# The order of transposes and gates within a chunk of a hybrid decoder's first stage

## The chip, the cores and the metric

The kernel runs on one core of one Trainium2 chip. The metric is the time of one execution on the device in microseconds, as the median of several runs. The core has a matrix engine (TensorE, PE in the rows; PEld is its weight load), a vector engine (VectorE, DVE), an activation engine (ScalarE, ACT), GpSimd (POOL) and SyncE (SP), which here issues all transfers. Each engine works through its own queue in order.

## What is computed

The reference is one inference step of one decoder layer with two groups of heads beside each other. For a prompt of 4096 positions with 1024 features (and 8 sample rows with one position each):

```
xn    = rms_norm(x, norm_pre)
proj  = xn @ w_in                    # 2304 columns, split into
x_rnn, g_rnn, q, k, v, g_att = split(proj)
xc    = causal_conv(x_rnn)           # width 4, per channel
r, i  = sigmoid(blockdiag(w_ga, xc) + b_ga), sigmoid(blockdiag(w_gx, xc) + b_gx)
a     = exp(-8 r softplus(-lam))
h_t   = a_t h_{t-1} + sqrt(1 - a_t^2) (i_t xc_t)
mix   = concat(h * silu(g_rnn), window_attention(q, k, v) * silu(g_att))
y     = x + rms_norm(mix @ w_out, norm_post)
```

Also returned are the last states of the convolution, the recurrence and the attention window. All is in float32; the kernel splits each operand of a product into a high and a low part and adds three products of them.

## The kernel before, in words

The work has three stages. **Stage A** does the norm, the transposes of the features, the projections of the recurrent half (eight tiles of 128 columns of `w_in`), the convolution, the gates and the scan. **Stage B** does the other projections and the attention, **stage C** the output projection. A and B go over the prompt in 11 chunks: the first has 256 positions and the 8 sample rows, the other ten 384 positions. The change lies in stage A alone.

Within stage A a chunk is a list of items, written out in `A_ORDER` (line 32) and worked off by the loop at lines 429 to 448. With `ci` the chunk and `c` one of the four channel tiles of the recurrent half:

- `P c` is `proj_A` (line 277): two projections side by side, the input and the SiLU gate of channel tile c (`project2`, line 190, with `mm3`, lines 123 to 125): 8 tiles of features, 2 outputs, 3 products, so 48 matmuls over 384 columns into two PSUM tiles of the tag `mm`, which has four. ACT then reads the first one twice (`xr`, line 286, and `xc`, line 290), VectorE adds three taps (line 292) and splits the result (`xk`, lines 300 and 301; 2 buffers); ACT takes the tanh of the second (line 304) and VectorE makes `sg` of it (line 306; 5 buffers).
- `R c` is `rnn_A` (line 309): six gate matmuls from `xk` into the one PSUM tile `gt` (lines 123 to 125 with `gt` as output), four activations on ACT (lines 321, 322, 325, 326), four operations on VectorE (lines 327 to 330).
- `L` is `load_A` (line 146) of chunk ci+1: for three tiles of 128 positions a transfer (line 154; the tag `xs` has 4 buffers), a sum of squares on ACT (line 162), a power and a scaling on POOL (lines 142 and 167).
- `X c` is `prep_A` (line 171) of chunk ci+1 for the feature tiles 2c and 2c+1: three transposes into a PSUM tile each (line 177; the tag `t` has 2), the high part on ACT (`xh`, line 180), the low part on VectorE (`xl`, line 181), and both parts sent to DRAM for stage B (line 183). `xh` and `xl` have 12 buffers each, and a chunk holds 8.
- `S` is `scan_A` (line 333) of chunk ci-1: one square root over all four channel tiles on ACT (line 336), which needs another activation table than the tanh and the exponential, then on VectorE a product, a scan and the product with `sg` for each channel tile (lines 338, 340, 349), and the transfers of line 350.

The loop of stage A, cut to the items:

```
for ci in range(NCH):
    for item in A_ORDER:
        f, s = item[0], st[ci]
        c = int(item[1:] or 0)
        if f == "P":
            s["p", c] = proj_A(pa, ci, c, wA, s["x"])
        elif f == "R":
            ...
            s["r", c] = rnn_A(pa, ci, c, s["uu"], *s["p", c])
        elif f == "S":
            ...
            scan_A(pa, ci - 1, s["uu"], [s["r", c] for c in range(4)])
        elif ci + 1 < NCH:
            if f == "L":
                s["n"] = load_A(prep, ci + 1)
            else:
                ...
                prep_A(ci + 1, s["n"], (2 * c, 2 * c + 1), x)
```

The text's order is not the order of an engine's queue. The program is built in a `TileContext` with `schedule_with_timeline_sim=True` (line 1020): a planner plays the program through at build time, with durations of its own. On each engine it takes, among the instructions whose inputs and buffers are ready in that play, the one that stands earliest in the text. A later item thus fills a gap of an earlier one. The queues that come out are fixed, and the chip's real durations do not change them.

Where stage A ends, its PSUM and SBUF pools are given to stage B (lines 722 to 728); eight tiles of `w_in` for stage B take the buffers of stage A's weights, and two more those of the pool `pa_late`, which holds `hh` among others.

Of the kernel before, what the change touches and what calls it, by code (L numbers as in the profile page):

```python
# [28 lines left out]

A_ORDER = "P1 S L P0 P2 R1 X0 R0 P3 X1 R2 X2 R3 X3".split()

B_FIRST = "V Q0 K Q1 U00 U01 Q2 Q3 G0 U02 U10 G1 U11 U12 M00 M01 G2 G3 M02 X M10 M11 M12".split()
B_ORDER = "Q0 Q1 K Q2 V U00 U01 Q3 U02 U10 G0 U11 G2 G1 M00 M01 M02 U12 G3 M10 M11 M12 X".split()
# [9 lines left out]
def hymba_kernel(ctx: ExitStack, tc: tile.TileContext, ins, outs):  # L45
# [70 lines left out]
    def load_w_in(m, pool=None, bufs=None, spare=None, eng=nc.vector, fast=False):  # L116
        return load_w(w_in_v[:, :, m * P:(m + 1) * P], f"in{m}", pool or wpool, bufs, spare, eng, fast)
# [97 lines left out]

    AORDER = [m for item in A_ORDER if item[0] == "P" for m in (int(item[1]), 4 + int(item[1]))]
    wA = {m: load_w_in(m, eng=nc.gpsimd, fast=True) for m in AORDER[:2]}
# [211 lines left out]
# [3 lines that stand above are left out]
# [603 lines left out]
```

## Time and profile before

| | us |
|---|---|
| median of 3 runs | 1421.48 (1420.98 to 1422.85) |
| the profiled execution's own time | 1416.61 |
| span of the profiled execution | 1414.5 |
| PE busy in the span | 1366.8 (97%) |
| VectorE busy | 1023.1 (72%) |
| ACT busy | 829.9 (59%) |
| POOL busy | 445.0 (31%) |

Stage A lies between about 15 and 463 us of the span, stage B begins beside its end, and stage C ends at 1414.5 us. All tables of the section on rows are of this one execution. "Busy" of PE counts pipelined matmuls up to their modelled ends, so a matmul's duration (0.33 us) is about twice its distance to the next.

### The profile page before, as it was taken

The numbers are of one execution on the slowest core, as the hardware profiler recorded it, in microseconds if no ns is written. First come the engines' busy times: TensorE is split into PE (matmuls) and PEld (weight loads), VectorE is DVE, ScalarE is ACT, GpSimd is POOL, SyncE is SP. The second block draws the span as 40 slices with busy tenths as digits, with TensorE's granted clock in tenths as the row PEclk, the third lists the DMA queues.
The fourth block names the chain that finished last, engine by engine and source line by source line (L and its number), as shares of the span: only waits on it lengthen the run. The fifth ranks groups of instructions, "written<-read, shape, count | busy, mean of one in ns | idle before, by whom it ended". The sixth has DMA issues, their size and how long they took to land. (4 is left out here: it accounts for less than half of the span.)

```text
span 1414.5 us, 23962 instructions
## 1 busy us (share of the span) xinstructions
PE 1366.8 (97%) x7983; PEld 1290.1 (91%) x7983; DVE 1023.1 (72%) x2421; ACT 829.9 (59%) x2095; POOL 445.0 (31%) x876
## 2 busy tenths in 40 slices
PE   5999999999999879999999999999999999999998
PEld 4999989999999879999999999999998887788886
DVE  6778877878778776566576665665676798888874
ACT  4666656756656666676675775766777443333431
POOL 3233332223421023544543534545435110000000
PEclk9999999999999999999999999999999999999999
DMA  8423453433337430331312303303134665345542
GB/s 265 146 96 140 146 173 133 148 121 133 127 120 203 142 120 9 120 113 61 101 51 73 101 13 113 102 13 112 57 103 133 201 198 166 127 158 176 170 157 90
DMA packets 139013, 174.42 MB, mean 123 GB/s; under 512 B 12646, under 2 KB 120758, under 8 KB 138890
## 3 DMA queue, kind: packets, MB, share of 16 engines
q1 hardware_dynamic: 138890, 172.90, 37.5%
q8 instruction: 63, 1.03, 0.3%
q14 instruction: 60, 0.49, 0.1%
HBM read 104.38 MB, written 68.50 MB: 122 GB/s over the span
## 5 line engine op out<-in xcount | busy, mean ns | idle before, releaser
L124 PE MATMUL pr<-xl,wh_in 128*128 128x384 f32 (+1 forms) x688 | 229.7, 335 | 0.0
L125 PE MATMUL pr<-xh,wl_in 128*128 128x384 f32 (+1 forms) x688 | 227.8, 333 | 0.0
L123 PE MATMUL pr<-xh,wh_in 128*128 128x384 f32 (+1 forms) x688 | 218.1, 337 | 8.3 <-ACT xc L290 8.3
L123 PEld LDWEIGHTS pr<-xh,wh_in 128*128 128x128 f32 x688 | 128.1, 188 | 10.1 <-ACT xc L290 9.8
L606 ACT ACTIVATE tt<-tt,nm 128x129 f32<-128x129 f32 x256 | 99.9, 393 | 61.4 <-DVE nm L603 61.2
L124 PEld LDWEIGHTS pr<-xl,wh_in 128*128 128x128 f32 x688 | 129.4, 188 | 0.7 <-issue 0.7
L125 PEld LDWEIGHTS pr<-xh,wl_in 128*128 128x128 f32 x688 | 129.3, 188 | 0.0
L123 PE MATMUL pq<-xh_B,wh_in 128*128 128x384 f32 (+1 forms) x352 | 117.7, 335 | 1.8 <-ACT qz L550 1.1
L123 PE MATMUL pga<-xh_B,wh_in 128*128 128x384 f32 (+1 forms) x352 | 118.3, 336 | 0.7 <-ACT qz L550 0.7
L124 PE MATMUL pga<-xl_B,wh_in 128*128 128x384 f32 (+1 forms) x352 | 118.0, 335 | 0.0
L124 PE MATMUL pq<-xl_B,wh_in 128*128 128x384 f32 (+1 forms) x352 | 117.9, 335 | 0.0
L125 PE MATMUL pq<-xh_B,wl_in 128*128 128x384 f32 (+1 forms) x352 | 117.9, 335 | 0.0
L125 PE MATMUL pga<-xh_B,wl_in 128*128 128x384 f32 (+1 forms) x352 | 117.2, 333 | 0.0
L292 DVE SCALAR_TENSOR_TENSOR xc<-xr,cT,xc 128x384 f32<-128x384 f32 (+1 forms) x132 | 87.3, 677 | 6.8 <-ACT xc L290 6.5
L633 POOL TENSOR_SCALAR_AFFINE_SELECT p<-ph 64x256 fp32r<-64x256 f32 x124 | 53.1, 429 | 103.0 <-PE po L640 82.1
L123 PEld LDWEIGHTS pq<-xh_B,wh_in 128*128 128x128 f32 x352 | 66.8, 190 | 2.4 <-ACT qz L550 1.4
L655 POOL TENSOR_TENSOR mxb<-mxb,sgb 128x256 f32<-128x256 f32 x64 | 47.1, 741 | 67.3 <-DVE mxb L648 64.0
L321 ACT ACTIVATE thr<-gt,hba 128x384 f32<-128x384 f32 (+1 forms) x44 | 25.2, 573 | 72.3 <-PE gt L125 71.4
L123 PEld LDWEIGHTS pga<-xh_B,wh_in 128*128 128x128 f32 x352 | 66.7, 190 | 0.9 <-ACT qz L550 0.9
L125 PEld LDWEIGHTS pq<-xh_B,wl_in 128*128 128x128 f32 x352 | 66.9, 190 | 0.3 <-issue 0.2
L124 PEld LDWEIGHTS pq<-xl_B,wh_in 128*128 128x128 f32 x352 | 66.9, 190 | 0.1
L124 PEld LDWEIGHTS pga<-xl_B,wh_in 128*128 128x128 f32 x352 | 66.8, 190 | 0.0
(764 smaller groups left out, 4100.2 us busy)
## 6 DMA issues: line engine op xcount, KB each, us to landing
xs<-in_x_prompt_dram SPq DMA_DIRECT2D x32, 512.0 KB
xr<-in_x_prompt_dram SPq DMA_DIRECT2D x32, 512.0 KB
out_dram<-xr SPq DMA_DIRECT2D x31, 512.0 KB
xT_d<-xh SPq DMA_DIRECT2D x80, 192.0 KB
xT_d<-xl SPq DMA_DIRECT2D x80, 192.0 KB
xh_B<-xT_d SPq DMA_DIRECT2D x80, 192.0 KB
xl_B<-xT_d SPq DMA_DIRECT2D x80, 192.0 KB
mix<-mix_d SPq DMA_DIRECT2D x30, 512.0 KB
```

Of the source, the lines that this page charges most:

```text
L123: nc.tensor.matmul(out, wh, xh, start=first, stop=False)
L124: nc.tensor.matmul(out, wh, xl, start=False, stop=False)
L125: nc.tensor.matmul(out, wl, xh, start=False, stop=last)
L292: nc.vector.scalar_tensor_tensor(xc[:, :npt], xr[:, t:t + npt], cw[:, t, c:c + 1], xc[:, :npt], op0=ALU.mult, op1=ALU.add)
L321: act(thr, pg[:, 0:W], AF.Tanh, scale=0.5, bias=hba[:, c:c + 1])
L606: act(tt[:, g, 0:P + 1], tt[:, g, 0:P + 1], AF.Exp, scale=-1.0, bias=nm[:, g:g + 1], accum_out=sm[:, g:g + 1])
L633: nc.gpsimd.affine_select(dst, src[r, :, r], pattern=[[0, 4], [-1, HD]], compare_op=ALU.is_gt, fill=0.0, base=0, channel_multiplier=1)
L655: nc.gpsimd.tensor_mul(oo, oo, st["sg", kv][:, :, b * P:(b + 1) * P])
```

## The change

Only the order of the items changes. P1 S L P0 P2 stays; X0 goes ahead of R1, X1 ahead of R0, X2 and X3 stand around P3 where R0, X1 and R2 stood, and R2 and R3 come last.

```diff
-A_ORDER = "P1 S L P0 P2 R1 X0 R0 P3 X1 R2 X2 R3 X3".split()
+A_ORDER = "P1 S L P0 P2 X0 R1 X1 R0 X2 P3 X3 R2 R3".split()
```

`AORDER` (line 216), the order in which stage A's weights are loaded, is taken from the P items and stays 1, 0, 2, 3. For the last chunk X and L are empty.

## Rows read from the trace of the kernel before

**Rows 1.** The page, part 1: busy time and share of the span, by engine.

```profile
PE 1366.8 (97%) x7983; PEld 1290.1 (91%) x7983; DVE 1023.1 (72%) x2421; ACT 829.9 (59%) x2095; POOL 445.0 (31%) x876
```

**Rows 2.** Busy time by stretches: one chunk, and the handover to stage B.

```profile
core 0: us, PE busy (x) PEld busy (x) DVE busy (x) ACT busy (x) POOL busy (x), PEclk, DMA share, GB/s
...
239.60:279.70 40.10, 40.07 (x238) 39.83 (x239) 33.47 (x67) 25.91 (x44) 10.27 (x18) 1.00 0.39 137
...
470.00:515.00 45.00, 32.16 (x213) 29.83 (x212) 37.04 (x101) 32.69 (x84) 3.17 (x9) 0.89 0.17 53
```

**Rows 3.** Waits of PE, 40 to 440 us: us in total, times, longest.

```profile
PE pr L123 <- ACT xc L290: 6.8, 5, 1.6
PE pt L177 <- POOL xs L167: 0.4, 1, 0.4
```

**Rows 4.** Timeline around one stall: start, us, engine, line, operation [idle before].

```profile
400.07 1.28 ACT L336 ACT_TABLE_LOAD   x1
...
401.36 1.49 ACT L336 ACTIVATE uu<-uu 128x1536 f32<-128x1536 f32 x1
...
403.79 0.47 ACT L286 ACTIVATE xr<-pr 128x384 f32<-128x384 f32 x1
404.16 0.66 ACT L290 ACTIVATE xc<-pr,cT 128x384 f32<-128x384 f32 x1
...
404.88 0.44 PE L123 MATMUL pr<-xh,wh_in 128*128 128x384 f32 x1 [1.58 <-ACT xc L290]
```

**Rows 5.** Timeline of PE around the end of a chunk's P3, before that stall.

```profile
371.36 0.42 PE L123 MATMUL pr<-xh,wh_in 128*128 128x384 f32 x1
...
380.89 0.82 PE L177 MATMUL pt<-ident,xs 128*128 128x128 f32 x6
...
392.66 0.34 PE L123 MATMUL gt<-xk,gwh 128*128 128x384 f32 x1
...
395.09 0.49 PE L177 MATMUL pt<-ident,xs 128*128 128x128 f32 x3
```

**Rows 6.** Timeline of PE: six transposes between matmuls of a projection.

```profile
229.34 0.82 PE L177 MATMUL pt<-ident,xs 128*128 128x128 f32 x6
229.92 0.42 PE L124 MATMUL pr<-xl,wh_in 128*128 128x384 f32 x1
230.18 0.33 PE L125 MATMUL pr<-xh,wl_in 128*128 128x384 f32 x1
```

**Rows 7.** Groups of ACT, 40 to 440 us.

```profile
L180 ACT ACTIVATE xh<-pt,gpre 128x384 fp32r<-128x384 f32 x80 | 43.8, 584 | 22.0 <-PE pt L177 22.0
...
L326 ACT ACTIVATE thr<-thr,sp4n 128x384 f32<-128x384 f32 (+1 forms) x40 | 28.1, 702 | 0.9
...
L321 ACT ACTIVATE thr<-gt,hba 128x384 f32<-128x384 f32 (+1 forms) x40 | 22.9, 572 | 72.2 <-PE gt L125 71.4 <-DVE xl L181 0.7
```

**Rows 8.** Groups of VectorE, 40 to 440 us.

```profile
L292 DVE SCALAR_TENSOR_TENSOR xc<-xr,cT,xc 128x384 f32<-128x384 f32 (+1 forms) x117 | 78.1, 685 | 6.8 <-ACT xc L290 6.5 <-POOL xh L288 0.2
L181 DVE SCALAR_TENSOR_TENSOR xl<-pt,gpre,xh 128x384 fp32r<-128x384 f32 x80 | 47.6, 611 | 11.7 <-ACT xh L180 11.5
```

**Rows 9.** Timeline of SP's queue: loads of three tiles for a later chunk.

```profile
353.01 1.31 SPq L154 DMA_DIRECT2D xs<-in_x_prompt_dram  x3
```

**Rows 10.** Timeline of POOL: scaling of the second of those tiles.

```profile
366.08 1.84 POOL L167 TENSOR_SCALAR xs<-xs,rs 128x1024 f32<-128x1024 f32 x1
```

**Rows 11.** Timeline of VectorE: the first product with `sg` in a chunk's scan.

```profile
409.46 1.12 DVE L349 TENSOR_TENSOR hh<-hh,sg 128x384 f32<-128x384 f32 x1
```

**Rows 12.** Timeline of PE at the handover: waits of over 2 us.

```profile
475.32 0.44 PE L123 MATMUL gt<-xk,gwh 128*128 128x384 f32 x1 [2.86 <-ACT thi L322]
...
504.63 0.66 PE L614 MATMUL pT<-ident,tt 128*128 128x128 f32 x4 [2.24 <-DVE tt L611]
...
508.82 0.77 PE L623 MATMUL po<-ph,vs 128*128 128x512 f32 x1 [3.53 <-ACT ph L618]
```

**Rows 13.** Timeline of ACT at the handover: the wait ahead of two weight tiles.

```profile
506.09 2.00 ACT L112 ACTIVATE wh_in<-ws_in 128x1024 fp32r<-128x1024 f32 x2 [3.69 <-DMA mix_d<-hh]
```

## The prediction

> **What bounds the kernel now.** The page first: PE is busy for 97% of the span [rows 1], so only its idle time and the small costs between its matmuls can be won, 47.7 us in all. The next view is the busy time by stretches. It shows where this idle time is not: a chunk of stage A without a stall lasts 40.1 us and PE is busy in 40.07 of them, at the full granted clock (1.00, 2.4 GHz) [rows 2]. It is also not in POOL or SP, which PE hardly ever waits for.
>
> The waits of PE between 40 and 440 us then say what ends its idle time in the middle of stage A: 6.8 us in front of projections, five waits released by ACT's `xc`, and 0.4 us in front of transposes, released by POOL [rows 3].
>
> The timeline of the longest shows the mechanism [rows 4]. PE waits at 404.88 for a PSUM tile that `xr` and `xc` still read. These stand in ACT's queue behind the square root of the scan and its table load (400.07 to 402.85). That alone would not matter: a projection pair has two of four `mm` tiles, so while P0 runs, P1's are read. But here P1 and P0 end together, so all four are full. The reason is in PE's timeline [rows 5]. P3 of the old chunk ends at 380.89, and only then do X1's six transposes run; X3's last three run at 395.09, 14.2 us after P3. Until then P1 lacks its last feature tiles, P0 is taken as filler with what is there, and both finish after X3.
>
> **The change, part by part.** Write c for a chunk. Nothing is added or removed: per chunk 192 projection matmuls, 24 gate matmuls, 24 transposes, and the same work on every other engine, four transfers on SP for each X included.
>
> *X0 to X2 go ahead of P3, X3 right behind it.* X0 needs the scaled tiles `xs`. Their loads are issued at 353.01, when X3 has read the tiles before, and the second of them is scaled by 367.92, 14.9 us later [rows 9, 10]; the first two X's of the next chunk would now be due 25 us and more after X3, so the 0.4 us POOL wait goes too. In P3's window PE has 48 + 12 (R1, R0) matmuls at 0.176 us (54 took the 9.53 us from 371.36 to 380.89 [rows 5]) and three X's of 0.58 us [rows 6], 12.3 us. ACT has in it six `xh`, eight activations of R1 and R0 (at 0.57 and 0.70) and P2's reading: 3.5 + 5.1 + 1.6 = 10.2 us [rows 4, 7]. VectorE has six `xl` (3.7 us), three taps (2.1 us) and eleven other passes over a tile of the same size; taking each at the 0.61 us of `xl`, too much rather than too little, 6.7 us: 12.5 us [rows 8]. So VectorE is about full, and X2 and X3 may slip a little behind P3. `xh` and `xl` of X2 and X3 also need buffers that P3 is the last to read (12 for 8 + 8), which come free tile by tile as P3 goes. I take X3 as done 2 us after P3.
>
> *What follows for P1 and P0.* With all feature tiles there, P1 takes its 48 matmuls first, R2 and R3 among them, and ends some 11 us after P3; P0 ends 8.4 us later. In these 8.4 us ACT has to read P1's tiles. At worst the root stands ahead of it with both table loads, 2 x 1.28 + 1.49 = 4.1 us, then `xr` and `xc`, 1.1 us [rows 4]: 5.2 us, so P2 finds its tiles free. X3 would have to be done later than about 8 us after P3 to bring the stall back. Taken out: all five stalls, -6.8 us; bounds 0 and -6.8. With the POOL wait, -0.4.
>
> The page "ScalarE: Activation LUTs" of the Trainium skill, section "What ACT_TABLE_LOAD costs", speaks against this ease: it gives a table switch 2.66 us, the load and a drain. By it the root's block would be an estimated 6.8 us, with `xr` and `xc` 7.9, and hardly anything of P0's 8.4 us would be left, so that one sum of squares in between would keep part of each stall and the sum would lose up to some 6 us. The rows show the load alone: the root starts 1.29 us after its load began [rows 4], and I go by that.
>
> *Transposes between matmuls.* Six take 0.58 us wherever they stand, and the matmul behind them 0.42 us in place of 0.33 [rows 6]: 0.09 us for each return to matmuls. X0 now comes in two or three pieces and would come in one, X1 to X3 may come in three to six. One return less in two of three chunks, out of nine, is -0.5 us; bounds -1.5 and +1.5.
>
> *R2 and R3 last.* R0 now runs after P3 and R3's first matmul at 392.66, 11.8 us after it [rows 5]. With R1 and R0 inside P3, R3 waits only for P3's own taps, about 6 us. So the scan's start comes about 6 us sooner. The gates' own cost, 24 x 0.176 us, does not change, and P1 covers R3's wait.
>
> *The handover to stage B.* In the last chunk there is no X, but P1 there still ends with P0, and all four gates come behind P3. One of them is waited for (2.86 us), and the first attention units wait 2.24 and 3.53 us [rows 12], the last one because ACT stands before a weight tile whose buffer the scan's output holds until it is sent, 3.69 us [rows 13]. PE is idle for 12.8 of 45 us there, and the clock is at 0.89 on average, so part of the stretch ran at the lower level, 1.2 GHz [rows 2]. With P1 early, R1 and R0 move into P3, and the last scan follows P3 sooner. How much of the idle time goes, no row shows, as VectorE is busy for 37.0 of the 45 us: bounds -8.6 us (those three waits) and +3.5 us (one more such wait). I take half of the gain, -4.0, as the gate wait goes first.
>
> **The sum.** -6.8 - 0.4 - 0.5 - 4.0 = -11.7 us. Against the profiled execution, 1416.61 us in a span of 1414.5, this is 1404.9 us. The median of the runs, 1421.48, lies 4.9 us above that execution; with the same difference the median is 1409.8 us, -0.8%. A measurement can tell about 0.2%, 2.8 us, from no change.
>
> **The rivals.**
> *The handover gives all it has*, the three waits of 8.6 us: -16.3 us, 1405.2 us. For it speaks that all three hang on the last gates and the scan; against it, VectorE's load.
> *The stalls stay*: if the planner, with durations of its own, places X3 still 8 us or more behind P3, P1 and P0 end together as before. For it speaks that the planner spaces gates widely, ACT waits 71 us for them [rows 7], and that VectorE is nearly full in P3's window. Then the handover stays too, and the time is about 1421 us.
> *A smaller stall stays*: the root with its two loads and a sum of squares end up ahead of `xr` and `xc`, and each takes longer than its row. If P2 still waits 0.6 us in nine chunks, that is 5.4 us given back, 1415.2 us. The rows speak against it, with 5.2 of 8.4 us [rows 4]. The page's 2.66 us for a switch would bring it about.
> *Slower, a new wait at P3's first matmul.* `sg` has five buffers, so P0's takes the place of one that the last scan must have multiplied. That product starts at 409.46, 28.6 us after P3 [rows 5, 11]; with P0's own pass at 0.6 us its PSUM tile is free at about 29.8 us. In the new order P3 is due after 156 matmuls and six transposes, 28.0 us. If the scan came no sooner than now, P3 would wait 1.8 us in nine chunks, 16.2 us; less the 7.2 us of stalls, 1430.5 us. It decides where R3, now behind X3 and R2 in the text, gains less than 1.8 us; I count on 6.
>
> **How the numbers follow.** Forecast 0.52, handover in full 0.14, smaller stall 0.05, stalls stay 0.17, new wait 0.12. The forecast's own range, with the bounds of the returns and the handover, is 1404 to 1418 us. The range reaches from 1403 to 1421 us, over the first four cases, and leaves out the slower one. Faster by over 0.2% are the first three, 0.71; within it the fourth, 0.17; slower the last, 0.12.
>
> **What would show it.** Right: no wait of PE on `xc` between 40 and 440 us; X1 and X2 inside P3 and X3 within 3 us of its end; P1's 48 matmuls done well before P0's; chunks of 40 us throughout. R3 within 7 us of P3, and at the handover no gate wait. Wrong: transposes still 7 us or more behind P3; a wait of P3 or P2 on `sg`, line 306; idle time after 470 us as long as now or longer, whatever the chunks do.

## The result, and the profile after

The changed kernel takes 1405.47 us (median of 5 runs, 1400.21 to 1407.19) against 1421.48 us before: 16.0 us less, a ratio of 0.9877 with a 95% interval of 0.9862 to 0.9893. Forecast were 1409.8 us in a range of 1403 to 1421, so the sign is right and the size 4.3 us short. The profiled execution took 1400.21 us with a span of 1398.5, against 1416.61 and 1414.5 before, so the two spans, 16.0 us apart, may be compared: each is the fastest execution on record of its kernel.

The page, part 1, of the changed kernel (busy time, share of the span, instructions):

```profile
PE 1364.4 (98%) x7983; PEld 1292.2 (92%) x7983; DVE 1016.5 (73%) x2421; ACT 829.8 (59%) x2095; POOL 463.5 (33%) x876
```

PE's busy time has hardly changed, 1364.4 against 1366.8 us [rows 1]; what went is mostly idle time, 34.1 in place of 47.7 us. Where it went is seen by cutting both spans at two places: the end of the last projection of stage A (462.6 us before, 453.0 after), and the first scores of stage B's second chunk (538.9 and 521.9). I call the piece between them the handover. Busy time by stretches, of the kernel before and then of the changed one; the columns are us, PE, PEld, DVE, ACT, POOL, PE's granted clock, DMA share, GB/s:

```profile
40.00:462.60 422.60, 415.39 (x2488) 409.52 (x2487) 330.46 (x668) 262.56 (x453) 127.99 (x188) 1.00 0.42 142
462.60:538.90 76.30, 63.32 (x418) 60.30 (x418) 53.93 (x137) 48.51 (x123) 13.88 (x32) 0.93 0.34 109
```

```profile
40.00:453.00 413.00, 412.82 (x2477) 408.82 (x2477) 325.30 (x669) 264.53 (x454) 144.55 (x187) 1.00 0.44 146
453.00:521.90 68.90, 60.51 (x421) 59.41 (x420) 50.51 (x131) 44.78 (x118) 13.62 (x31) 0.95 0.36 115
```

Stage A ends 9.6 us sooner. PE's idle time in it is 0.2 us in place of 7.2. The handover is 7.4 us shorter: PE's idle time falls from 13.0 to 8.4 us there, and the granted clock rises from 0.93 to 0.95. Of the 17.0 us won by then, 1.0 comes back in the stages behind. There the clock of this execution is at 0.51 from 1060.6 to 1064.0 us, with PE busy for 3.35 of the 3.4 us, which costs it 1.7 us; between 538.9 us and the last 3 us of the kernel before it never falls.

The waits of PE between 40 and 440 us (us in total, times, longest), where five stalls on `xc` stood [rows 3]:

```profile
PE pr L123 <- DVE sg L306: 0.2, 1, 0.2
```

The stalls and the POOL wait are gone. The one wait left, 0.2 us on `sg`, is at the place of the prediction's slower rival.

PE's timeline around the end of a chunk's P3, in the changed kernel (start, us, engine, line, operation), to be held against [rows 5]:

```profile
374.48 0.82 PE L177 MATMUL pt<-ident,xs 128*128 128x128 f32 x6
375.05 0.42 PE L125 MATMUL pr<-xh,wl_in 128*128 128x384 f32 x1
375.31 0.34 PE L123 MATMUL gt<-xk,gwh 128*128 128x384 f32 x1
...
380.04 0.49 PE L177 MATMUL pt<-ident,xs 128*128 128x128 f32 x3
...
380.90 0.49 PE L177 MATMUL pt<-ident,xs 128*128 128x128 f32 x3
...
382.62 0.34 PE L123 MATMUL gt<-xk,gwh 128*128 128x384 f32 x1
```

X2 lies inside P3, whose last matmul is at 375.05 and which ends at 375.31, where R2 follows. X3 runs at 380.04 and 380.90, and R3 begins at 382.62. X3's last three transposes come 5.6 us after P3's end, where they came 14.2 us after it. From 384.75 us on PE runs 106 projection matmuls without a break. Of these 12 are P1's and 46 P0's, so P1 ends a whole 8 us ahead of P2.

ACT's timeline in the same chunk shows what became of the block that held `xr` back [rows 4]:

```profile
385.15 1.06 ACT L162 ACTIVATE sq<-xs 128x1024 bf16<-128x1024 f32 x1 [3.14 <-DMA xs<-in_x_prompt_dram]
...
387.73 0.49 ACT L286 ACTIVATE xr<-pr 128x384 f32<-128x384 f32 x1
388.10 0.68 ACT L290 ACTIVATE xc<-pr,cT 128x384 f32<-128x384 f32 x1
...
390.64 1.06 ACT L162 ACTIVATE sq<-xs 128x1024 bf16<-128x1024 f32 x1 [0.88 <-DMA xs<-in_x_prompt_dram]
...
391.81 1.28 ACT L336 ACT_TABLE_LOAD   x1
393.10 1.50 ACT L336 ACTIVATE uu<-uu 128x1536 f32<-128x1536 f32 x1
394.55 0.49 ACT L286 ACTIVATE xr<-pr 128x384 f32<-128x384 f32 x1
```

P1's tile is read at 387.73, 5.4 us before the root (393.10), and only P0's stands behind it. The sums of squares `sq` (line 162) still wait for the loads of the raw tiles, 3.14 us here and 30.8 us between 40 and 440 us against 12.1 before; from 40 us on PE waits for nothing behind them any more.

The waits of PE in the handover, 453.0 to 521.9 us:

```profile
PE pga L123 <- ACT qz L550: 3.7, 1, 3.7
PE pga L123 <- DVE sgb L561: 3.2, 2, 2.7
PE pq L123 <- DVE ksT L510: 1.5, 1, 1.5
```

The three long waits of [rows 12], 8.6 us, and ACT's wait of [rows 13] are gone. Beside them stood 4.3 us of other waits; now these others are 8.4 us.

### The profile page after: what moved, and what is told of

Same layout as the page of the kernel before. It is cut to its first block, busy times and chain, and to the rows that moved or that the text cites. A ratio compares the mean times of both kernels' runs of the same rounds, so it can differ in the third digit from the quotient of the medians.

```text
span 1398.5 us, 23988 instructions
## 1 busy us (share of the span) xinstructions
PE 1364.4 (98%) x7983; PEld 1292.2 (92%) x7983; DVE 1016.5 (73%) x2421; ACT 829.8 (59%) x2095; POOL 463.5 (33%) x876
## 5 line engine op out<-in xcount | busy, mean ns | idle before, releaser
L123 PE MATMUL pr<-xh,wh_in 128*128 128x384 f32 (+1 forms) x688 | 227.1, 334 | 1.1 <-ACT xc L290 0.9
L283 POOL COPY xr<-xh 128x3 f32<-128x3 f32 x40 | 49.5, 1239 | 125.4 <-DVE xc L292 98.5
L292 DVE SCALAR_TENSOR_TENSOR xc<-xr,cT,xc 128x384 f32<-128x384 f32 (+1 forms) x132 | 80.5, 611 | 11.6 <-POOL xh L288 7.4
L180 ACT ACTIVATE xh<-pt,gpre 128x384 fp32r<-128x384 f32 (+1 forms) x88 | 47.4, 576 | 51.3 <-PE pt L177 51.1
L619 DVE TENSOR_TENSOR pl<-pT,ph 128x512 fp32r<-128x512 f32 x64 | 44.0, 688 | 33.1 <-PE po L640 23.4
```

What stands on the lines that cost most here:

```text
L123: nc.tensor.matmul(out, wh, xh, start=first, stop=False)
L180: act(h, pt[:, :W], AF.Copy, scale=gpre[:, k:k + 1])
L283: nc.gpsimd.tensor_copy(xr[:, 0:3], xrprev[c])
L292: nc.vector.scalar_tensor_tensor(xc[:, :npt], xr[:, t:t + npt], cw[:, t, c:c + 1], xc[:, :npt], op0=ALU.mult, op1=ALU.add)
```

## The experiments

My theory after the result: the stalls went because X3 comes early, so that P1 ends ahead of P0; and the handover gained because the last chunk's P1 ends early, which chunk 9's order sets. Each run below is compared with the kernel before; runs 3, 6, 7, 8, 9, 11 and 12 are edits of the changed kernel, the others of the kernel before. Times are medians over executions, but waits and stretches are those of the one profiled execution. The handover of runs 6 and 7, whose chunks have the changed kernel's order, takes 70.2 and 69.8 us in place of 68.9, so I read nothing into a difference of 1 to 2 us.

**1. The gates alone.**

```diff
-A_ORDER = "P1 S L P0 P2 R1 X0 R0 P3 X1 R2 X2 R3 X3".split()
+A_ORDER = "P1 S L P0 P2 R1 X0 R0 P3 X1 X2 X3 R2 R3".split()
```

> Only R2 and R3 are put behind X2 and X3; the X items keep their places of before, so X3 still ends some 13 us after P3 (88 matmuls and transposes behind it) and P1 and P0 end together. Theory (it is the transposes' places that count): stalls of P2 on xc as before, 5 to 9 us in all, the handover as before, time 0.997 to 1.003 of the kernel before. Rival (it is the gates' places that count): stalls gone and the scan sooner, 0.995 or less.

Measured: 1414.47 us, ratio 0.9949 (0.9933 to 0.9964); three stalls, 3.9 us in all; handover 74.7 us. Neither theory has this: the stalls stay, and yet 6.7 us are won. Where these lie stays open. The trace can't say, as the profiled execution was the slowest of the ten (1420.72 us, 4.1 us more than that of the kernel before), and in it stage A ends 2.9 us later than before although the stalls are 2.9 us shorter.

**2. One item alone.**

```diff
-A_ORDER = "P1 S L P0 P2 R1 X0 R0 P3 X1 R2 X2 R3 X3".split()
+A_ORDER = "P1 S L P0 P2 R1 X0 R0 X1 P3 R2 X2 R3 X3".split()
```

> One item alone moves from the order of before: X1 goes from behind P3 to ahead of it. X3 then ends 53 matmuls and transposes after P3 (36 in the changed kernel, 84 to 88 before) and P1 ends 33 of them, some 6 us, ahead of P2. Theory: 6 us are enough for the root's block of 5.2 us, so the stalls are gone or below 1.5 us, and the handover gains as P1 of the last chunk is early too; 0.987 to 0.992 of the kernel before. Rival (X2 ahead of P3 and the gates behind are needed): stalls of 3 us or more stay, 0.994 or more.

Measured: 1408.87 us, ratio 0.9900 (0.9875 to 0.9924). One wait on `xc` of 0.3 us is left and stage A ends at 454.6 us. The handover takes 74.7 us: at most 1.6 us of the 7.4 are there. So X1 ahead of P3 is enough for 8.0 of stage A's 9.6 us, and the early end of P1 in the last chunk is not enough for the handover.

**3. The order of before in chunk 9.**

```diff
+A_OLD = "P1 S L P0 P2 R1 X0 R0 P3 X1 R2 X2 R3 X3".split()
...
-        for item in A_ORDER:
+        for item in A_OLD if ci == NCH - 2 else A_ORDER:
```

> The changed order in every chunk but 9, which has the order of before; chunk 9 makes the feature tiles of the last chunk, so P1 and P0 end together there and the gates of the last chunk come behind P3. Theory: the gain of stage A's chunks stays (8 to 9.5 us), that of the handover (7.4 us) goes, as it hangs on P1 of the last chunk: 0.993 to 0.995 of the kernel before, with the gates of R3 15 us or more behind P3's end. Rival (the handover gains because stage A ends sooner and its queues are emptier, whatever chunk 9 does): 0.987 to 0.990.

Measured: 1414.83 us, ratio 0.9939 (0.9915 to 0.9963). No stall on `xc` after the first chunk, and the handover, by busy time:

```profile
457.60:536.00 78.40, 64.26 (x412) 61.46 (x411) 52.73 (x133) 47.81 (x123) 12.81 (x31) 0.91 0.32 103
```

78.4 us: the whole gain of the handover is gone, as the theory said, and the clock with it, 0.91. The changed order in chunk 9 is needed for it.

**4. A root without a table.** The scan's root is replaced by a scaled copy, so the root is left out of what is computed.

```diff
-        act(uu[:, :, :W], uu[:, :, :W], AF.Sqrt, scale=-0.25)
+        act(uu[:, :, :W], uu[:, :, :W], AF.Copy, scale=-0.25)
```

> The kernel before, with the scan's square root replaced by a scaled copy, which needs no table of its own (the root is left out of what is computed); PE's order in the chunks is that of before, X3 still 13 us behind P3. Theory (stalls come from xr and xc behind the root and its two table loads, once P1 and P0 end together): the block is some 2.6 us shorter, the stalls were at most 1.6 us each, so they are gone or below 1 us in all, and the handover gains 0 to 3 us; 0.993 to 0.996 of the kernel before. Rival (two projections that end together stall P2 by themselves): stalls of 5 us or more stay, 0.998 to 1.000.

Measured: 1416.21 us, ratio 0.9956 (0.9935 to 0.9977). The time is as expected, the stalls are not: three of five went, two stayed with 4.1 us, one of them longer (2.97 us) than any before. The 2.7 us of stalls are not all of the 4.9 us won; the rest stays open. At that place ACT shows what stands ahead of `xr`:

```profile
73.58 1.06 ACT L162 ACTIVATE sq<-xs 128x1024 bf16<-128x1024 f32 x1 [2.67 <-DMA xs<-in_x_prompt_dram]
74.55 0.19 ACT L162 ACTIVATION_READ_ACCUMULATOR sq<-xs 128x1 f32 x1
74.64 0.47 ACT L286 ACTIVATE xr<-pr 128x384 f32<-128x384 f32 x1
```

No root, but a sum of squares that waits 2.67 us for its load. The root alone is not the cause. In the kernel before, the stall at this place (1.27 us, at 72.38) looks the same: the root is done at 66.97, and between it and `xr` stand two sums that wait for loads.

```profile
68.33 1.06 ACT L162 ACTIVATE sq<-xs 128x1024 bf16<-128x1024 f32 x1 [1.35 <-DMA xs<-in_x_prompt_dram]
...
70.23 1.06 ACT L162 ACTIVATE sq<-xs 128x1024 bf16<-128x1024 f32 x1 [0.76 <-DMA xs<-in_x_prompt_dram]
...
71.29 0.47 ACT L286 ACTIVATE xr<-pr 128x384 f32<-128x384 f32 x1
```

With this the stall of [rows 4] reads differently. SP's timeline and ACT's, in the kernel before, ahead of those rows:

```profile
395.43 0.81 SPq L154 DMA_DIRECT2D xs<-in_x_prompt_dram  x2
```

```profile
398.90 1.06 ACT L162 ACTIVATE sq<-xs 128x1024 bf16<-128x1024 f32 x1 [1.80 <-DMA xs<-in_x_prompt_dram]
...
402.75 1.04 ACT L162 ACTIVATE sq<-xs 128x1024 bf16<-128x1024 f32 x1
```

It is a chain that starts at X3. Its last transposes (395.09) free `xs`; the loads are issued at 395.43; the first sum of squares starts at 398.90, having waited 1.80 us for its load; behind it come the table load, the root and a second sum, and only at 403.79 `xr`. From X3's end at 395.34 to P2 at 404.88 that is 9.5 us, and PE had 8.0 us of work for them. In the changed kernel PE has 58 matmuls and more, 13.7 us, between X3 and P2.

**5. More buffers for the raw tiles**, to take the loads off X3.

```diff
-            xs = pool.tile([P, D], F32, tag="xs", name=f"xs_{ci}_{j}", bufs=4)
+            xs = pool.tile([P, D], F32, tag="xs", name=f"xs_{ci}_{j}", bufs=6)
```

> The order of before, with six buffers for the raw feature tiles xs in place of four, so that the loads of the next chunk's tiles need not wait until X3 has read the old ones; PE's order keeps X3 84 to 92 matmuls and transposes behind P3, and P1 and P0 still end together. Revised theory (what holds xr and xc back is a chain that starts at X3: it frees xs, the load then takes some 4 us, the sum of squares on ACT waits for it with the root and xr behind it): no sum of squares waits for a load after the first chunks, the stalls of P2 fall to below 2 us in all from 6.8, 0.994 to 0.997 of the kernel before. Rival (the root and its table load alone, with P1 and P0 ending together): stalls of 5 us or more stay, 0.998 to 1.002.

Measured: 1421.85 us, ratio 0.9998 (0.9984 to 1.0013), with four stalls of 8.7 us. This doesn't decide: the loads did not come sooner. SP's queue still issues them right behind X3 (356.69 us, X3's end at 356.5), so the edit didn't do what it was for.

**6. The slower rival's place: one `sg` less.**

```diff
-        sg = pal.tile([P, STEP], F32, tag="sg", name=f"sg_{ci}_{c}", bufs=5)
+        sg = pal.tile([P, STEP], F32, tag="sg", name=f"sg_{ci}_{c}", bufs=4)
```

> The changed order with four buffers for sg in place of five; PE's order in the chunks is that of the changed kernel. In the changed kernel P0's sg comes at 402.56, right behind the last scan's products (401.15 on), and P3 could start at 404.85, so the new wait of the slower case misses by some 2 us. With four buffers P1's sg takes the place of P1's of the last chunk, which is the second product's, about 401.7: P1's PSUM tiles, read out at 391.0 now, would be free at 402.3, and P2's first matmul, due at about 395, waits. Theory: PE waits on sg in front of P2 for 6 to 8 us in nine or ten chunks, 50 to 80 us in all, 1.035 to 1.055 of the kernel before. Rival (the scan's products are not what frees sg, or the scan comes earlier by itself): no wait over 1 us, 0.986 to 0.992.

Measured: 1404.81 us, ratio 0.9882 (0.9858 to 0.9905), and no wait of PE at all between 40 and 440 us. A clear miss. P1's `sg` did come late, as the VectorE rows of this run say, 403.06 in place of 390.42:

```profile
401.48 1.66 DVE L349 TENSOR_TENSOR hh<-hh,sg 128x384 f32<-128x384 f32 x3
403.06 0.55 DVE L306 SCALAR_TENSOR_TENSOR sg<-thg,pr 128x384 f32<-128x384 f32 x1
404.05 0.55 DVE L306 SCALAR_TENSOR_TENSOR sg<-thg,pr 128x384 f32<-128x384 f32 x1
```

But P2 didn't need P1's second tile. In PE's queue of this kernel P2 does 23 matmuls of its first half before the second half begins, where the changed kernel alternates by threes. It begins at 399.71, and by then `xc` has read P0's first tile (396.52). The other three of the four tiles are still held then, by P2's first half and by the two `sg` above, so P2's second half must have taken that one. The planner had moved the wait away, so the price of a late `sg` is lower than I had it.

**7. The transposes alone.**

```diff
-A_ORDER = "P1 S L P0 P2 X0 R1 X1 R0 X2 P3 X3 R2 R3".split()
+A_ORDER = "P1 S L P0 P2 X0 R1 X1 R0 X2 P3 R2 X3 R3".split()
```

> The transposes as in the change, but R2 stays between P3 and X3 and R3 behind it, so the gates are not put behind X3. In the chunks PE's order comes out as in the changed kernel. Theory (the second half of the change, the gates behind, does nothing): as the changed kernel, 0.984 to 0.991 of the kernel before, no stall on xc after the first chunk and the handover 68 to 71 us. Rival (gates behind X3 are needed, as the run with them alone gained 0.5%): 0.992 or more.

Measured: 1402.57 us, ratio 0.9862 (0.9844 to 0.9880), the same within the intervals as the changed kernel; no stall on `xc` after the first chunk, handover 69.8 us. With the transposes ahead, R2 may stand ahead of X3 or behind it: PE's queue in the chunks comes out the same.

**8. All transposes within P3.**

```diff
-A_ORDER = "P1 S L P0 P2 X0 R1 X1 R0 X2 P3 X3 R2 R3".split()
+A_ORDER = "P1 S L P0 X0 P2 X1 R1 X2 R0 X3 P3 R2 R3".split()
```

> A try at more: X0 stands behind P0, X1 to X3 between P2 and P3's end, R2 and R3 last, so that X3 ends with P3 and four groups of six transposes remain in place of five. Theory: one return to matmuls less, 0.1 to 0.2 us in nine chunks, and the xs loads come 5 us sooner, which nobody waits for any more: 0 to 2 us better than the changed kernel in the chunks; the handover, where R3 of the last chunk comes five matmuls later, within 2 us of the changed kernel's: 0.984 to 0.990 of the kernel before. Rival (P0's sg, which has 2 us to spare in the changed kernel, becomes the bound, as P1's work ends sooner while the scan doesn't): waits on sg of 1 us or more in most chunks, 0.992 or more.

Measured: 1405.81 us, ratio 0.9892 (0.9876 to 0.9908): no better than the changed kernel. There is no wait on `sg`; the handover takes 71.2 us, and an X0 waits 0.9 us for POOL at 76.5 us. With X3 early enough, earlier gives nothing.

**9. The changed order in chunk 9 alone**, the loop of the third run with the two orders exchanged.

```diff
-        for item in A_ORDER:
+        for item in A_ORDER if ci == NCH - 2 else A_OLD:
```

> The complement of the third run: the changed order in chunk 9 alone, the order of before in all others. X3 of the last chunk then ends 59 matmuls and transposes behind P3 (36 in the changed kernel, 86 before) and P1 of the last chunk ends 30 ahead of P0. Theory (the handover hangs on chunk 9): four or five stalls on xc stay in chunks 1 to 8, and the handover, from the last matmul of P3 to the third group of 16 scores, takes 69 to 74 us in place of 76.5: 0.994 to 0.998 of the kernel before. Rival (it hangs on the chunks before, through the scans and loads that they leave behind): handover 76 us or more, 0.998 to 1.001.

Measured: 1417.19 us, ratio 0.9968 (0.9952 to 0.9984); the stalls stay, five with 8.5 us, and the handover is:

```profile
468.90:542.00 73.10, 63.33 (x423) 61.11 (x422) 52.28 (x135) 44.79 (x118) 13.80 (x31) 0.93 0.36 113
```

3.2 us of the 7.4 come from chunk 9 alone. The planner places X3 of chunk 9 later in this kernel (59 matmuls and transposes behind P3) than in the changed one (36). Over all runs the handover goes with this number: 68.9 to 70.9 us with 36 (the changed kernel and runs 6, 7, 11 and 12), 71.2 with X3 inside P3 (run 8), 73.1 and 74.7 with 59 and 53 (runs 9 and 2), 74.3 to 78.4 with 77 to 89 (the rest). By which wait it does so is not shown.

**10. Without the sums of squares.** From chunk 2 on, ones stand in their place, so the features are not normalised by row.

```diff
-                act(sq[:rows], xs[:rows], AF.Square, scale=1.0 / 32.0, accum_out=ss[:rows])
+                act(sq[:rows], xs[:rows], AF.Square, scale=1.0 / 32.0, accum_out=ss[:rows]) if ci < 2 else nc.vector.memset(ss[:rows], 1.0)
```

> The order of before, with the sums of squares of chunks 2 to 10 left out (ones stand in their place, so the features are not normalised by row). ACT then has three passes less in a chunk and waits for no load of raw features; the root and its table load stay, and PE's order keeps X3 83 to 88 matmuls and transposes behind P3. Theory (the block in front of xr and xc is a chain from X3: load, sum of squares, table load, root, sum of squares, 9.4 to 9.9 us in the rows, against 7 to 9 us from X3 to P2): without load and squares 2.8 us are left and the stalls of P2 after 120 us are gone or below 0.6 us each, 0.994 to 0.997 of the kernel before. Rival (the root alone holds them back): stalls of 1 us or more in three chunks or more after 120 us, 0.998 or more.

Measured: 1410.10 us, ratio 0.9921 (0.9902 to 0.9941), more than expected. The waits of PE between 40 and 440 us, and ACT around the root in this kernel:

```profile
PE pt L177 <- POOL xs L167: 1.8, 2, 1.2
```

```profile
391.04 1.28 ACT L336 ACT_TABLE_LOAD   x1
392.51 1.49 ACT L336 ACTIVATE uu<-uu 128x1536 f32<-128x1536 f32 x1 [0.18 <-DVE uu L329]
395.17 0.49 ACT L286 ACTIVATE xr<-pr 128x384 f32<-128x384 f32 x1 [1.17 <-PE pr L125]
```

Every stall on `xc` is gone, with the root and its table load in place, and with X3 78 to 88 matmuls and transposes behind P3 (77 to 90 in the kernel before). ACT now waits 1.17 us for PE. The chain from X3 over load and squares was the cause, and the root only a part of its length. This run takes out the wait for the load and the squares' own time together; it doesn't say which of the two counts for more.

**11. VectorE's load at the handover**, a try at more.

```diff
-            wB[m] = load_w_in(m) if len(wB) < 8 else load_w_in(m, pbl, 2)
+            wB[m] = load_w_in(m, eng=nc.gpsimd) if len(wB) < 8 else load_w_in(m, pbl, 2, eng=nc.gpsimd)
```

> A try at more, on the changed order: the low parts of stage B's ten weight tiles are made on POOL in place of VectorE. In the changed kernel nine of them lie between 430 and 525 us, 1.22 us each, 11.0 us, while VectorE is busy nearly without a gap from 439 to 484 us and POOL idles. On POOL one takes 3.14 us, as at the kernel's start. Theory (VectorE's load sets the handover): the last gates and the scan come some 4 to 6 us sooner, the handover takes 62 to 67 us in place of 69.1, 0.983 to 0.988 of the kernel before, 2 to 6 us below the changed kernel. Rival (PSUM tiles and ACT set it, or POOL's passes slow VectorE's down): handover 68 us or more, 0.987 or more.

Measured: 1413.80 us, ratio 0.9952 (0.9937 to 0.9966), 8 us worse than the changed kernel. The handover itself takes 69.4 us, but the loss lies ahead of it: the last chunk's P3 waits on `sg`. PE's timeline, and the groups of VectorE from 430 to 525 us, in this kernel (busy us, mean ns of one):

```profile
452.60 0.69 PE L123 MATMUL pr<-xh,wh_in 128*128 128x384 f32 x1 [6.79 <-DVE sg L306]
```

```profile
L292 DVE SCALAR_TENSOR_TENSOR xc<-xr,cT,xc 128x384 f32<-128x384 f32 x12 | 16.0, 1330 | 3.6 <-ACT xc L290 3.5
L340 DVE TENSOR_TENSOR_SCAN hh<-aa,hl,thi 128x384 f32<-128x384 f32 x8 | 9.7, 1263 | 0.0
L349 DVE TENSOR_TENSOR hh<-hh,sg 128x384 f32<-128x384 f32 x8 | 6.1, 817 | 0.0
```

The same groups in the changed kernel:

```profile
L340 DVE TENSOR_TENSOR_SCAN hh<-aa,hl,thi 128x384 f32<-128x384 f32 x8 | 7.8, 1002 | 0.0
L292 DVE SCALAR_TENSOR_TENSOR xc<-xr,cT,xc 128x384 f32<-128x384 f32 x11 | 6.6, 607 | 0.0
L349 DVE TENSOR_TENSOR hh<-hh,sg 128x384 f32<-128x384 f32 x8 | 4.2, 547 | 0.0
```

With POOL's subtractions running, a tap takes 1330 in place of 607 ns on average, a scan 1263 in place of 1002, a product 817 in place of 547. VectorE was relieved of 11.0 us and lost more in slower passes: 12 x 0.72 + 8 x 0.26 + 8 x 0.27 = 12.9 us in these groups alone. And the slower rival's wait exists: with the scan late P3 stands for 6.79 us, and from 450.2 to 457.1 us the clock is at 0.51. Stage A ends at 463.1 us in place of 453.0.

**12. An earlier gate projection in stage B**, a second try.

```diff
-B_FIRST = "V Q0 K Q1 U00 U01 Q2 Q3 G0 U02 U10 G1 U11 U12 M00 M01 G2 G3 M02 X M10 M11 M12".split()
+B_FIRST = "V Q0 K Q1 G0 U00 U01 Q2 Q3 U02 U10 G1 U11 U12 M00 M01 G2 G3 M02 X M10 M11 M12".split()
```

> A try at more, on the changed order: in the first chunk of stage B the item G0 (one gate projection, 24 matmuls, 4.2 us, read by one pass of ACT and one of VectorE) goes ahead of the first attention units, from behind Q3, so that PE has work while the last scan keeps ACT and VectorE busy. In the changed kernel PE idles there for 8.4 us, 3.7 us ahead of G0 (until ACT's qz) and 2.7 us ahead of the second gate projection. Theory (PE only lacks work that the others don't have to serve): one of the two waits goes, the handover takes 65 to 68 us in place of 69.1, 1 to 4 us below the changed kernel, 0.983 to 0.988 of the kernel before. Rival (ACT and VectorE are full, and what is moved forward is missing later): the waits move to Q2, Q3 or the units, the handover takes 69 us or more, 0.986 to 0.991.

Measured: 1406.76 us, ratio 0.9900 (0.9881 to 0.9919), handover 70.9 us. The wait moved, as the rival said:

```profile
485.98 0.47 PE L580 MATMUL S<-kt,sq 128*128 128x128 f32 x1 [6.00 <-DVE sq L545]
```

Two single waits, 3.7 and 2.7 us, became one of 6.00 us. No version beat the changed kernel by more than the intervals.

## Why the prediction was right, and where it was not

**The stalls, -6.8 us: right, for half a reason.** All five went, and the POOL wait too, so these terms hold. The mechanism named, the root and its table loads ahead of `xr`, was only part of it (runs 4 and 10). What I left out is the load of the raw tiles, which X3 releases, and the sums of squares that wait for it in ACT's queue. The row of the load's wait lay next to the rows I had read; I began reading at the table load. The same omission makes the bound "X3 later than 8 us after P3" one about the wrong pair of events: what counts is the time from X3 to P2, which was 8.0 us of work for a chain of 9.5, and is 13.7 now.

**Transposes and the rest of stage A, -0.5 us: too small.** Stage A's end came 9.6 us sooner; 7.0 us are waits, 1.0 us came in chunk 0 (its wait on `xc` is 0.93 us in place of 1.53, its P2 starts at 35.99 in place of 36.97), and 1.6 us remain, just outside the bounds of 1.5 either way. Where they come from stays open. Fewer returns to matmuls are not shown as their cause: between 40 and 440 us the transposes stand in 53 groups in place of 74, but in run 2 they stand in 81, and its chunks without a wait take 40.2 us too.

**The handover, -4.0 us: the mis-sized term.** It gave 7.4 us. "I take half of the gain" had no row behind it. The rival that took it in full was nearest, with 1405.2 us, but not by its reason: its three waits did go, but the other waits grew from 4.3 to 8.4 us. Of the 7.4 us, 4.6 are idle time. A further part is the clock, a term that I had read and not used. These are the stretches of the handover at the lower level (1.2 GHz), of the kernel before and then of the changed one:

```profile
476.60:480.00 3.40, 3.40 (x18) 3.40 (x17) 3.40 (x9) 2.60 (x5) 0.00 (x0) 0.50 0.53 155
507.30:514.10 6.80, 4.59 (x17) 3.93 (x18) 4.39 (x8) 6.62 (x23) 0.20 (x1) 0.50 0.02 4
```

```profile
480.40:487.20 6.80, 6.22 (x29) 6.22 (x29) 4.49 (x24) 2.71 (x9) 0.00 (x0) 0.50 0.32 117
```

PE was busy at half the clock for 8.0 us before and for 6.2 us now, so the clock gave back an estimated 0.9 us, half of the difference; the other 1.9 us no row separates. Of R1 and R0, which were to move into P3, only R1 did: 7 of the last chunk's 24 gate matmuls lie ahead of the last projection, where none did before. Runs 3 and 9 show that chunk 9's order is needed for the gain and gives 3.2 us of it alone; run 2 shows that an early P1 is not enough. Why the gain is 7.4 us stays open, and that the total came near this rival's is luck in part.

**The sum.** The four pieces are 7.0 us of waits and 2.6 us besides in stage A, 7.4 us at the handover, and 1.0 us given back behind it, for which the sum had no term. The prediction's own range was also added up wrongly: with the bounds of the returns and the handover its upper end is 1419.3 and not 1418 us. The wider range, to 1421 us, covers this.

**The smaller steps.** X1 and X2 lie inside P3: right. X3 within 3 us of P3's end: wrong, 5.6 us, and no stall came of it. R3 within 7 us: 7.3. P1 well before P0: right. No gate wait at the handover: right. "Chunks of 40 us throughout": seven of the nine full chunks that still make transposes take 40.1 to 40.2 us, from P3 to P3; the other two take 42.7 (with the extra matmuls of lines 376 and 390 in it) and 41.0 us.

**The slower rival.** The wait on `sg` was the right place: 0.2 us once in the changed kernel, 6.79 us in run 11. The sum for it was off twice. The scan's first product comes 24.9 us after P3 (375.31 to 400.18), 3.7 us sooner and not 6. But P3 is due 29.5 us after the last (404.85), not 28.0, since 162 matmuls and twelve transposes lie between, where 156 and six were counted. So P0's tile, free at 403.1 us, has 1.7 us to spare. Run 6 shows besides that the planner can move such a wait away.

**The rival from the page "ScalarE: Activation LUTs"** of the Trainium skill (section "What ACT_TABLE_LOAD costs") has not come about: after the load at 391.81 us the root starts at 393.10, again 1.29 us later.

## What to carry to other kernels

When an engine releases a wait late, read its queue back to the first instruction that itself waited for something: here a wait "on `xc`" was one for a load, issued when another engine's work had freed its buffer. Moving one producer (X1) ahead of P3 gave most of stage A's gain (run 2); with the transposes ahead, the gates' places added nothing that can be measured (run 7), though alone they gave 0.5% whose place is open (run 1). Where a stretch is bound by several engines in turn, as the handover is, moving single pieces of work about (runs 8, 11, 12) won nothing, and in run 12 the wait only came back under another name.

## What the hardware showed that was not expected

VectorE does not slow down evenly beside POOL, it stands. In run 11 two taps, 0.61 us each otherwise, take 1.86 and 2.74 us, and end 0.4 us after the end of POOL's subtraction beside them (430.47 and 433.61 us). VectorE's timeline and then POOL's:

```profile
429.03 1.86 DVE L292 SCALAR_TENSOR_TENSOR xc<-xr,cT,xc 128x384 f32<-128x384 f32 x1 [2.03 <-ACT xc L290]
...
431.28 2.74 DVE L292 SCALAR_TENSOR_TENSOR xc<-xr,cT,xc 128x384 f32<-128x384 f32 x1
```

```profile
428.07 2.40 POOL L113 TENSOR_TENSOR wl_in<-ws_in,wh_in 128x1024 fp32r<-128x1024 f32 x1 [6.54 <-ACT wh_in L112]
...
430.90 2.71 POOL L113 TENSOR_TENSOR wl_in<-ws_in,wh_in 128x1024 fp32r<-128x1024 f32 x1
```

The Trainium skill's page "SBUF — State Buffer", section "Who interferes with whom", says that a VectorE instruction with two SBUF inputs contends with a GpSimd (POOL) instruction that reads SBUF, and that the later of the two blocks until the first is done. Taps, scans and products have two such inputs, and the trace agrees: both times POOL's subtraction began first (428.07 ahead of 429.03, 430.90 ahead of 431.28).

A stall early on can cost more than its own time. In run 1 a wait of 2.32 us at 36 to 38 us is followed by a stretch at the lower clock (columns as above):

```profile
38.00:40.00 2.00, 1.56 (x9) 1.56 (x10) 1.93 (x8) 2.00 (x6) 2.00 (x4) 0.78 0.05 20
40.00:42.00 2.00, 2.00 (x11) 2.00 (x10) 2.00 (x9) 1.88 (x4) 0.60 (x4) 0.50 0.00 0
42.00:44.00 2.00, 2.00 (x17) 2.00 (x16) 1.96 (x12) 0.82 (x2) 1.13 (x4) 0.87 0.00 0
```

Here 1.7 us go to the clock on top of the wait (2 us each at 0.22, 0.50 and 0.13 below full, with PE busy nearly throughout). It doesn't always happen: in run 12 a wait of 2.71 us at the same place left the clock at 1.00 between 24 and 60 us.
